# Reordering the state-space stages with a third Toeplitz buffer, moving a copy from GpSimd to ScalarE, and a later softmax sum in a hybrid decoder layer

## The chip, the core and the metric

The kernel runs on one core of a Trainium2 chip. The metric is the device time in microseconds (us) of one execution. Engines are called by the names of the profile: PE is the matmul engine (PEld its weight load), DVE the vector engine, ACT the scalar engine, POOL is GpSimd, and SP issues the transfers.

## The reference, cut to what matters

One decoder layer of 1024 tokens and width 1024. An input projection feeds three token mixers and their gates; then come cross attention and a SwiGLU. Two of the mixers matter here.

```
# forgetting attention, 8 heads x 64
s = q k^T * scale + c_q - c_k          # causal
p = softmax(s);  out = p @ v
# diagonal state space (S5), 32 groups of 16 channels, 64 complex states
drive = u @ bbar;  h = scan(abar, drive);  y = Re(h @ c) + d * u
z = gelu(y);  out = z * sigmoid(z @ w_glu + b_glu)
```

All is float32. Large matmuls are done with each operand split in a high part (fp32r) and the rest, so one product is three matmuls (high x high, high x low, low x high).

## The kernel before, in words

The program is written as generators that a planner interleaves. A stage that has to run in order (the "driven" one) issues a piece of its work; after each piece the planner issues ("pumps") some microseconds of filler matmuls, which are projection blocks `pj` from a list of jobs. Each filler block is 48 matmuls of 512 columns, with weights that SP loads (`wr`), ACT rounds to the high part (`wh`) and DVE turns into the low part (`wl`), one to two blocks ahead. Driven stages are given a priority some instructions ahead of the fillers (60 for S5, 10 for the attention, 20 for work put off with `later`). The order on each engine is fixed when the program is built, by that priority and by when inputs are expected to be there; on the chip each engine takes its instructions in that order and waits where one is not ready. Nearly all tiles come from one arena of 50 buffers of 128 x 1024 floats; an instruction that opens a new tile has to wait for the last reader of the buffer's former tile.

**S5.** `s5_main` walks 8 octets of channels through four stages. `s5_prep` (POOL) makes the tables X and Z1 and loads the inputs U; `s5_prep2` makes rotation tables on DVE (CO, SI), transposes X on PE (`s5g`), makes the short kernel (`s5k`), and SP writes it with 8 transfers into a block Toeplitz matrix (`toep`); `s5_body` projects (`s5d`), rotates and scans on DVE and leaves the carried states in `kcs`; `s5_out` multiplies Toeplitz x U and Z1 x `kcs` on PE (`s5y`), then does the gelu on DVE and ACT and stores. In step o of the loop octet o is in prep, o-3 in out, o-1 in prep2 and o-2 in body, issued in this order, with 4.5, 5.4, 2.7 and 4.5 us of filler after each (S5_US = 4.5 times a weight). `toep` and `kcs` have two buffers each.

**Attention.** `fox_main` runs 16 units (4 pairs of heads, 2 halves of the queries, 2 heads) of 4 or 8 key blocks, 96 blocks in all. A block's scores `st` (PE) go through Exp on ACT to `pf`; POOL copies `pf` to the high part of `pt`; DVE subtracts to get the low part; POOL adds `pf` into the row sums `facc`; two matmuls `pv` follow two blocks later. The maxima of the next unit's scores are found meanwhile (`mx` on PE, reductions on DVE to `mc`, transposes `mt` on PE, q tables `q12a`/`q12b` on ACT). At the end of a unit `fox_out` splits `facc` into `ah` (ACT, then DVE); after the second head of a pair a routine put off by 2.0 us sums `ah` over the partitions on PE (`sm`).

Of the kernel before, what the change touches and what calls it, by code (L numbers as in the profile page):

```python
# [13 lines left out]
AF = mybir.ActivationFunctionType  # L14
ALU = mybir.AluOpType
# [51 lines left out]
HG_LAT = 5.0  # L67
FOXL_W = 10.0
FOXL_T = 8.0
EPS = 1e-6  # L70
NEG = -1e30
HG_LEVELS = (1, 2, 4, 8, 16)
# [116 lines left out]
class Trunk:  # L189
# [538 lines left out]
                out.append(piece(i, c))  # L728
        return out + [chain, rows]

    hi_pool = (0, 1, 2, 3)

    def fox_main(self):
        units = self.fox_units()
        pend = deque()
        pre = self.fox_pre(units[0])
        for i, f in enumerate(pre):
            f()
            yield FOX_P[i >= len(pre) - 3]

        def drain(n):
            while len(pend) > n:
                pend.popleft()()

        for ui, un in enumerate(units):
            p, half, h = un
            self.unit = ui
            pre = self.fox_pre(units[ui + 1]) if ui + 1 < len(units) else []
            nj = 4 * half + 4
            per = [[] for _ in range(nj)]  # L750
            if pre:
                body, tail = pre[:-2], pre[-2:]
                w = nj - PRE_END[half]
                per[0].append(body.pop(0))
                b = BUILD[half]
                for i, f in enumerate(body):
                    per[min(b + i * (w - b) // len(body), w - 1)].append(f)
                per[w - 1].append(tail[0])
                per[nj - 1].append(tail[1])
            acc = self.u("facc")[:, 0:512]  # L760
            st = {}
            pf = None
            for j in range(nj):
                q0 = max(0, 128 * j - 512 * half)
                ps = self.psm("st")
                diag = j >= 4 * half
                self.mm(ps[:, q0:512], self.k1[h][:, 128 * j:128 * j + 128], self.q1[h][:, q0:512], True, False)
                self.mm(ps[:, q0:512], self.k2[h][:, 128 * j:128 * j + 128], self.q2[h][:, q0:512], False, not diag)
                if diag:
                    self.mm(ps[:, q0:q0 + 128], self.ident_r, self.mkq_r, False, True)  # L770
                if j % 2 == 0:
                    pf = self.u("pf").rearrange("p (a b) -> p a b", a=2)
                pr = pf[:, j % 2, q0:512]
                self.act(pr, ps[:, q0:512], AF.Exp)
                pt = self.u("pt", F32R).rearrange("p (a b) -> p a b", a=2)
                if j % 4 in self.hi_pool:
                    self.ts(pt[:, 0, q0:512], pr, 1.0, 0.0, ALU.mult, ALU.add, self.nc.gpsimd)
                else:
                    self.act(pt[:, 0, q0:512], pr, AF.Copy)
                self.sub(pt[:, 1, q0:512], pr, pt.bitcast(F32)[:, 0, q0:512])  # L780
                if j == 0:
                    p0 = pr
                elif j == 1:
                    self.add(acc[:, q0:512], p0[:, q0:512], pr, self.nc.gpsimd)
                    if q0:
                        self.ts(acc[:, 0:q0], p0[:, 0:q0], 1.0, eng=self.nc.vector)
                else:
                    self.add(acc[:, q0:512], acc[:, q0:512], pr, self.nc.gpsimd)

                def pv(j=j, q0=q0, pt=pt, un=un, st=st, nj=nj, acc=acc):  # L790
                    p, half, h = un
                    if j == 0:
                        st["o"] = self.psm("pv")
                    for i in range(2):
                        self.mm(st["o"][:, q0:512], self.vst[j][:, 256 * p + 128 * h:256 * p + 128 * h + 128], pt[:, i, q0:512],
                                start=j == 0 and i == 0, stop=j == nj - 1 and i == 1)
                    if j == nj - 1:
                        self.fox_out(un, st["o"], acc)
                pend.append(pv)
                drain(PV_LAG)  # L800
                for f in per[j]:
                    f()
                yield (0.5 + 0.5 * (512 - q0) / 512) * HALF_W[half] * (FOX_E[j - nj] if j >= nj - 2 else 1.0)
        while pend:
            yield 0.5
            drain(len(pend) - 1)
        yield

    def fox_out(self, un, o, acc):
        p, half, h = un  # L810
        b = 64 * h
        s, so = slice(b, b + 64), slice(64 - b, 128 - b)
        hs = slice(512 * half, 512 * half + 512)
        hd = 2 * p + h
        if half == 0 and h == 0:
            self.fy[p] = self.u(f"fy{p}")
        t = self.u("ft")
        self.act(t[s, 0:512], o[so], AF.Copy)
        self.add(self.fy[p][s, hs], o[s], t[s, 0:512])
        ah = self.u("ah", F32R).rearrange("p (a b) -> p a b", a=2)  # L820
        self.split(acc, ah[:, 0], ah[:, 1])

        self.fah.append((hd, ah))

        def sums():
            ps = self.psm("sm")
            todo, self.fah = self.fah, []
            for n, (hd_, a_) in enumerate(todo):
                for i in range(2):
                    self.mm(ps[0:8], self.ohc_r[:, hd_, 0:8], a_[:, i], start=n + i == 0,  # L830
                            stop=n == len(todo) - 1 and i == 1)
            if p == 0:
                self.nc.vector.tensor_copy(out=self.fsum[0:8, hs], in_=ps[0:8])
            else:
                self.add(self.fsum[0:8, hs], self.fsum[0:8, hs], ps[0:8])
        if h == 1:
            self.later(2.0, sums)
        if half == 1 and h == 1:
            self.nc.sync.dma_start(out=self.fy_d[p], in_=self.fy[p])

# [53 lines left out]
    def s5_params(self):  # L894
# [86 lines left out]
        t = tiny()  # L981
# [89 lines left out]
        for n in (1, 3):  # L1071
            fill(ear, eai, 1, n, n + 1)
        self.ear, self.eai, self.eb = ear, eai, eb

        tz, kz = self.u("toep"), self.u("kcs")
        G.memset(tz, 0.0)
        G.memset(kz, 0.0)
        self.toep, self.kcs = ([t[:, 512 * i:512 * i + 512].rearrange("p (g c) -> p g c", g=4) for i in range(2)]
                               for t in (tz, kz))
        self.s5t = tmv  # L1080
        self.s5d, self.r8 = rv[:, 768:800], rv[:, 800:832]
        G.tensor_copy(out=self.s5d, in_=prm[:, 96:128])
# [36 lines left out]
    def s5_prep2(self, o):  # L1119
        nc = self.nc  # L1120
        g0 = 4 * o
        gs = slice(g0, g0 + 4)
        d = self.s5o[o]
        ut, xt, X, Z1 = (d[k] for k in ("ut", "xt", "X", "Z1"))
        cx = self.cx

        def bh(t):
            return t[:, gs].unsqueeze(3).to_broadcast([P, 4, 8, 16])

        def bk(t):  # L1130
            return t[:, gs].unsqueeze(2).to_broadcast([P, 4, 8, 16])


        et = self.u("s5e")
        dt_ = self.u("s5dd")
        CO = et[:, 0:512].rearrange("p (g a j) -> p g a j", g=4, a=8)
        SI = et[:, 512:1024].rearrange("p (g a j) -> p g a j", g=4, a=8)
        tq = self.s5t[:, 1].rearrange("p (g a j) -> p g a j", g=4, a=8)
        ar, ai = bh(self.ear), bh(self.eai)
        br, bi = bk(self.eb[:, 0]), bk(self.eb[:, 1])  # L1140
        self.mul(CO, ar, br)
        self.mul(tq, ai, bi)
        self.sub(CO, CO, tq)
        self.mul(SI, ar, bi)
        self.mul(tq, ai, br)
        self.add(SI, SI, tq)

        gp = self.psm("s5g")
        for g in range(4):
            self.tp(gp[:, 128 * g:128 * g + 128], X[:, g].rearrange("p s h -> p (s h)"))  # L1150

        kp = self.psm("s5k")
        for g in range(4):
            x0 = X[:, g, 7]
            self.mm(kp[0:16, 128 * g:128 * g + 16], x0, cx[:, 0, g0 + g])
            self.mm(kp[0:16, 128 * g + 16:128 * g + 128], x0, Z1[:, g, 0:7].rearrange("p k h -> p (k h)"))
        G1 = xt[:, 0:512]
        self.act(G1, gp, AF.Copy)
        kt = ut[0:16, 512:1024]
        self.act(kt, kp[0:16], AF.Copy)  # L1160
        tz = self.toep[o % 2]
        ktv = kt.rearrange("p (g c) -> p g c", g=4)
        for s in range(8):
            nc.sync.dma_start(out=tz[16 * s:16 * s + 16, :, 16 * s:128], in_=ktv[:, :, 0:128 - 16 * s])
        d.update(et=et, dt=dt_, G1=G1.rearrange("p (g c) -> p g c", g=4), tz=tz)
# [56 lines left out]
    def s5_main(self):  # L1222

        self.s5o = {}
        for o in range(11):
            for lag, stage in ((0, self.s5_prep), (3, self.s5_out), (1, self.s5_prep2), (2, self.s5_body)):
                if 0 <= o - lag < 8:
                    stage(o - lag)
                    yield S5_W[lag] * (S5_END if o > 8 else S5_BEG if o < 2 else 1.0)
# [968 lines left out]
```

## Time and profile before

| | |
|---|---|
| median of 3 runs | 2164.51 us (2163.9 to 2166.4) |
| the profiled execution | 2162.11 us, span 2160.2 us |
| PE busy | 2101.3 us, 97% of the span |
| DVE / ACT / POOL busy | 1435.6 / 773.0 / 436.0 us |
| granted PE clock, mean | 0.995 |

The span is what the profiler saw from the first to the last instruction; 1.9 us of the execution lie around it. A busy time is the sum over instructions of an engine. S5 runs in the stretch up to about 325 us, the attention from there to about 632 us, and fillers run through both.

### The profile page before, as it was taken

The numbers are of one execution on the slowest core, as the hardware profiler recorded it, in microseconds if no ns is written. First come the engines' busy times: TensorE is split into PE (matmuls) and PEld (weight loads), VectorE is DVE, ScalarE is ACT, GpSimd is POOL, SyncE is SP. The second block draws the span as 40 slices with busy tenths as digits, with TensorE's granted clock in tenths as the row PEclk, the third lists the DMA queues.
The fourth block names the chain that finished last, engine by engine and source line by source line (L and its number), as shares of the span: only waits on it lengthen the run. The fifth ranks groups of instructions, "written<-read, shape, count | busy, mean of one in ns | idle before, by whom it ended". The sixth has DMA issues, their size and how long they took to land.

```text
span 2160.2 us, 26363 instructions
## 1 busy us (share of the span) xinstructions
PE 2101.3 (97%) x10176; PEld 1726.1 (80%) x10176; DVE 1435.6 (66%) x2193; ACT 773.0 (36%) x1208; POOL 436.0 (20%) x399
## 2 busy tenths in 40 slices
PE   8998999999999999999999999999999999989999
PEld 6887776776788888887888888878788888878887
DVE  8887898889845566536665577656877777743421
ACT  4113355545421222227243455444333333341200
POOL 4271204554531111001512000022211111100000
PEclk9999999999999999999999999999999999999999
DMA  4332220111210111124433433152222221272311
GB/s 164 137 99 73 51 86 20 42 47 32 77 63 20 50 69 54 64 108 175 146 104 140 185 98 119 58 184 99 88 88 88 88 80 69 86 273 83 117 58 55
DMA packets 74781, 201.87 MB, mean 93 GB/s; under 512 B 13337, under 2 KB 23065, under 8 KB 74657
## 3 DMA queue, kind: packets, MB, share of 16 engines
q1 hardware_dynamic: 74656, 200.20, 26.7%
q8 instruction: 80, 1.31, 0.2%
q14 instruction: 45, 0.36, 0.1%
HBM read 155.99 MB, written 42.99 MB: 92 GB/s over the span
## 4 chain that ended last, share of the span: by engine, by line
PE 67%; DVE 3%; issue 1%; ACT 1%; POOL 0%; DMA 0%; POOLq 0%; DVEq 0%; SPq 0%; ACTq 0%
PE pj L222 43%; PE fp L222 17%; PE hs L222 2%; PE xo L222 1%; PE xs L222 1%; PE rs L222 1%; PE ho L222 1%; POOL t L240 0%; PE hst L222 0%; DVE wl L240 0%; PE pv L222 0%; DMA wr<-xv 0%; PE st L222 0%; PE xt L227 0%; DVE tl L240 0%
## 5 line engine op out<-in xcount | busy, mean ns | idle before, releaser
L222 PE MATMUL pj<-xl,wh 128*128 128x512 f32 x784 | 315.2, 406 | 3.9 <-DVE xl L252 3.9
L222 PE MATMUL pj<-xh,wh 128*128 128x512 f32 x784 | 312.3, 403 | 6.5 <-ACT xh L237 5.6
L222 PE MATMUL pj<-xh,wl 128*128 128x512 f32 x784 | 311.4, 401 | 0.0
L240 DVE TENSOR_TENSOR wl<-wr,wh 128x1024 fp32r<-128x1024 f32 (+3 forms) x162 | 193.2, 1194 | 52.3 <-ACT wh L237 50.2
L222 PE MATMUL fp<-th,wc 128*128 128x512 f32 x640 | 208.2, 391 | 2.3 <-ACT th L237 2.3
L237 ACT ACTIVATE wh<-wr 128x1024 fp32r<-128x1024 f32 (+3 forms) x162 | 155.1, 960 | 142.1 <-PE pj L222 61.2
L240 DVE TENSOR_TENSOR xr<-pj,xr 128x512 f32<-128x512 f32 x80 | 54.8, 689 | 193.6 <-PE pj L222 188.1
L222 PEld LDWEIGHTS pj<-xh,wh 128*128 128x128 f32 x784 | 148.6, 190 | 39.0 <-ACT xh L237 6.0
L222 PEld LDWEIGHTS pj<-xl,wh 128*128 128x128 f32 x784 | 148.7, 190 | 36.0 <-DVE xl L252 6.1
L222 PEld LDWEIGHTS pj<-xh,wl 128*128 128x128 f32 x784 | 149.2, 190 | 31.0 <-issue 2.2
L222 PE MATMUL fp<-fx,wc 128*128 128x512 f32 x720 | 173.0, 389 | 0.0
L222 PEld LDWEIGHTS fp<-fx,wc 128*128 128x128 f32 x720 | 135.2, 188 | 28.1
L222 PEld LDWEIGHTS fp<-th,wc 128*128 128x128 f32 x640 | 121.0, 189 | 27.9 <-ACT th L237 2.7
L222 PE MATMUL pj<-hh,wl 128*128 128x512 f32 x352 | 134.4, 392 | 3.9 <-DVE wl L240 3.9
L222 PE MATMUL pj<-hh,wh 128*128 128x512 f32 x352 | 133.9, 391 | 1.6 <-ACT wh L237 1.6
L222 PE MATMUL pj<-hl,wh 128*128 128x512 f32 x352 | 133.8, 390 | 0.0
L222 PE MATMUL fp<-tl,wc 128*128 128x512 f32 x320 | 125.3, 392 | 1.5 <-DVE tl L240 1.5
L240 POOL TENSOR_TENSOR fc<-fc,fs 128x512 f32<-128x512 f32 x40 | 57.1, 1428 | 321.8 <-ACT fs L237 210.0
L240 DVE TENSOR_TENSOR pt<-pf,pt 128x512 fp32r<-128x512 f32 (+1 forms) x96 | 94.8, 990 | 39.6 <-POOL pt L256 39.3
L240 POOL TENSOR_TENSOR acc<-acc,sq 128x512 f32<-128x512 f32 (+1 forms) x18 | 30.7, 1707 | 375.8 <-ACT sq L237 375.7
L256 POOL TENSOR_SCALAR pt<-pf 128x512 fp32r<-128x512 f32 (+1 forms) x96 | 67.6, 705 | 139.1 <-ACT pf L237 127.8
L237 ACT ACTIVATE fs<-fc 128x512 f32<-128x512 f32 x40 | 25.3, 633 | 158.9 <-DVE fc L240 154.4
(415 smaller groups left out, 4744.4 us busy)
## 6 DMA issues: line engine op xcount, KB each, us to landing
wr<-w_in SPq DMA_DIRECT2D x48, 512.0 KB, 4.3
wr<-w_gu SPq DMA_DIRECT2D x44, 512.0 KB, 4.6
h_d<-fc SPq DMA_DIRECT2D x22, 512.0 KB, 2.9
hr<-h_d SPq DMA_DIRECT2D x22, 512.0 KB, 5.1
gz_d<-gz SPq DMA_DIRECT2D x20, 512.0 KB, 2.9
gate<-gz_d SPq DMA_DIRECT2D x20, 512.0 KB, 3.7
wr<-xo SPq DMA_DIRECT2D x17, 512.0 KB, 4.8
xr<-x_d SPq DMA_DIRECT2D x16, 512.0 KB, 6.2
```

What stands on the lines that cost most here:

```text
L222: self.nc.tensor.matmul(out, lhsT, rhs, start=start, stop=stop)
L237: self.nc.scalar.activation(out=out, in_=in_, func=f, **kw)
L240: return (eng or self.nc.vector).tensor_tensor(out=out, in0=a, in1=b, op=op)
L256: (eng or self.nc.vector).tensor_scalar(out=out, in0=a, scalar1=s1, scalar2=s2, op0=op0, **kw)
```

## The change

In `s5_main` the order within a step becomes prep (octet o), prep2 (o-1), out (o-3), body (o-2). The Toeplitz matrix of an octet goes to one of three buffers instead of two; the third is half of a new arena tile, `toep2`, cleared by POOL as the others are. In the attention the high part of `pt` is always copied by ACT (before, the set `hi_pool` sent all four residues of j, so every block, to POOL). The softmax sums are put off by 6.0 us instead of 2.0.

```diff
+SUM_AT = 6.0
...
-    hi_pool = (0, 1, 2, 3)
...
                 pt = self.u("pt", F32R).rearrange("p (a b) -> p a b", a=2)
-                if j % 4 in self.hi_pool:
-                    self.ts(pt[:, 0, q0:512], pr, 1.0, 0.0, ALU.mult, ALU.add, self.nc.gpsimd)
-                else:
-                    self.act(pt[:, 0, q0:512], pr, AF.Copy)
+                self.act(pt[:, 0, q0:512], pr, AF.Copy)
                 self.sub(pt[:, 1, q0:512], pr, pt.bitcast(F32)[:, 0, q0:512])
...
         if h == 1:
-            self.later(2.0, sums)
+            self.later(SUM_AT, sums)
...
-        tz, kz = self.u("toep"), self.u("kcs")
-        G.memset(tz, 0.0)
-        G.memset(kz, 0.0)
+        tz, tz2, kz = self.u("toep"), self.u("toep2")[:, 0:512], self.u("kcs")
+        for t in (tz, tz2, kz):
+            G.memset(t, 0.0)
         self.toep, self.kcs = ([t[:, 512 * i:512 * i + 512].rearrange("p (g c) -> p g c", g=4) for i in range(2)]
                                for t in (tz, kz))
+        self.toep.append(tz2.rearrange("p (g c) -> p g c", g=4))
...
-        tz = self.toep[o % 2]
+        tz = self.toep[o % 3]
...
-            for lag, stage in ((0, self.s5_prep), (3, self.s5_out), (1, self.s5_prep2), (2, self.s5_body)):
+            for lag, stage in ((0, self.s5_prep), (1, self.s5_prep2), (3, self.s5_out), (2, self.s5_body)):
```

## Rows read from the trace of the kernel before

**Rows 1.** The page, busy time, share of the span and instructions.
```profile
PE 2101.3 (97%) x10176; PEld 1726.1 (80%) x10176; DVE 1435.6 (66%) x2193; ACT 773.0 (36%) x1208; POOL 436.0 (20%) x399
```
**Rows 2.** Waits of PE, whole span: us in total, times, longest us.
```profile
PE s5y L222 <- DVE kcs L240: 10.1, 6, 3.3
PE sm L222 <- DVE ah L240: 8.1, 5, 2.3
PE mt L227 <- DVE mc L240: 7.8, 9, 1.7
...
PE st L222 <- ACT q12a L237: 1.4, 3, 0.6
...
PE pv L222 <- POOL pt L256: 0.5, 1, 0.5
```
**Rows 3.** Busy time of each engine by stretch, granted clock, DMA share.
```profile
150.00:325.00 175.00, 163.73 (x843) 133.42 (x843) 151.20 (x250) 66.51 (x94) 33.04 (x27) 0.98 0.25 70
325.00:640.00 315.00, 295.68 (x1415) 233.22 (x1414) 250.00 (x390) 160.11 (x269) 150.37 (x186) 0.99 0.14 46
```
**Rows 4.** PE in order of time around 170 us: start, us.
```profile
168.65 0.49 PE L222 MATMUL s5y<-kcs,s5x 128*128 128x128 f32 x2 [2.61 <-DVE kcs L240]
...
171.67 0.63 PE L222 MATMUL pj<-xl,wh 128*128 128x512 f32 x1
172.10 0.63 PE L222 MATMUL pj<-xh,wl 128*128 128x512 f32 x1
...
173.52 0.39 PE L222 MATMUL pj<-xh,wh 128*128 128x512 f32 x1
173.75 0.40 PE L222 MATMUL pj<-xl,wh 128*128 128x512 f32 x1
```
**Rows 5.** Two stretches of 25 us, columns as in rows 3.
```profile
200.00:225.00 25.00, 21.66 (x104) 18.24 (x103) 22.47 (x44) 5.79 (x11) 1.17 (x2) 0.93 0.10 20
...
500.00:525.00 25.00, 21.85 (x97) 16.81 (x96) 22.87 (x33) 11.26 (x19) 12.00 (x14) 0.93 0.08 22
```
**Rows 6.** PE in order of time: prep2 of one octet, and what follows it.
```profile
144.10 0.60 PE L227 MATMUL s5g<-cst,s5x 128*128 128x128 f32 x4
...
145.71 0.50 PE L222 MATMUL pj<-xl,wh 128*128 128x512 f32 x1
```
**Rows 7.** Waits of the SP queue, 60 to 370 us.
```profile
SPq L1164 <- PE s5y L222: 19.4, 3, 13.8
...
SPq L342 <- PE sm L222: 11.6, 1, 11.6
```
**Rows 8.** Waits of POOL, 140 to 325 us.
```profile
POOL s5x L240 <- DVE wl L240: 35.4, 1, 35.4
```
**Rows 9.** The page: costliest groups (busy us, mean ns), and a weight load's issue (us to landing).
```profile
L240 DVE TENSOR_TENSOR wl<-wr,wh 128x1024 fp32r<-128x1024 f32 (+3 forms) x162 | 193.2, 1194 | 52.3 <-ACT wh L237 50.2
...
L237 ACT ACTIVATE wh<-wr 128x1024 fp32r<-128x1024 f32 (+3 forms) x162 | 155.1, 960 | 142.1 <-PE pj L222 61.2
...
L256 POOL TENSOR_SCALAR pt<-pf 128x512 fp32r<-128x512 f32 (+1 forms) x96 | 67.6, 705 | 139.1 <-ACT pf L237 127.8
...
wr<-w_in SPq DMA_DIRECT2D x48, 512.0 KB, 4.3
```
**Rows 10.** Groups by shape, 325 to 632 us: busy us, mean ns, idle before.
```profile
L240 DVE TENSOR_TENSOR pt<-pf,pt 128x512 fp32r<-128x512 f32 x48 | 62.1, 1298 | 31.0 <-POOL pt L256 30.8
...
L240 DVE TENSOR_TENSOR ah<-facc,ah 128x512 fp32r<-128x512 f32 x16 | 11.8, 740 | 0.2
...
L237 ACT ACTIVATE ah<-facc 128x512 fp32r<-128x512 f32 x16 | 10.0, 626 | 0.7 <-DVE pt L240 0.5
...
L237 ACT ACTIVATE pf<-st 128x384 f32<-128x384 f32 x16 | 7.8, 486 | 17.5 <-PE st L222 17.5
...
L240 POOL TENSOR_TENSOR facc<-facc,pf 128x512 f32<-128x512 f32 x24 | 34.7, 1446 | 4.6 <-ACT pf L237 4.6
```
**Rows 11.** Waits of all engines, 325 to 640 us.
```profile
DVE pt L240 <- POOL pt L256: 39.3, 41, 3.5
```

## The prediction

> **What bounds the kernel now.** I began with the page: PE is busy 97% of the span [rows 1], so only its idle time, 2160.2 - 2101.3 = 58.9 us, and what a lower clock costs can be won; work taken off another engine wins nothing by itself. Then the waits of PE, to see whose they are [rows 2], and the table by stretch, to see where: S5 (150 to 325 us) leaves PE idle 175 - 163.7 = 11.3 us and the attention (325 to 640 us) 315 - 295.7 = 19.3 us [rows 3]. The change touches these two stretches and no other, so 30.6 us is the most that waits can give, plus the clock. The reader should see that three names make most of it: `s5y` waits for `kcs` (10.1 us), `sm` for `ah` (8.1), `mt` for `mc` (7.8). All three are ends of DVE chains, and DVE is busy 151.2 of 175 us (86%) in S5 and 250.0 of 315 (79%) in the attention [rows 3].
>
> A wait costs more than its length where the clock falls behind it. After PE stood 2.61 us for `kcs` the matmuls start 0.43 us apart (171.67 to 172.10), and 0.23 us apart again from 173.52 on [rows 4]; that is the lower of the two levels, 1.2 GHz. From the stretches with a granted clock of 0.93 [rows 5] such a dip costs about 25 x 0.07 = 1.75 us; that is two digits only, and I use 1.6. There are three: behind the 2.61 us wait, behind the longest `s5y` wait (3.3, in 200 to 225), and in 500 to 525, where I put it down to the longest `sm` wait.
>
> **The S5 order.** `s5y` of octet o-3 needs the `kcs` of the body one step earlier. Between the two the planner now puts 4.5 + 4.5 = 9.0 us of filler; with prep2 ahead of out it is 2.7 us more, plus prep2's own work on PE, 145.7 - 144.1 = 1.6 us [rows 6]: 4.3 us more distance, against a longest wait of 3.3. So all six should go. The body keeps its place in the step, and its chain on DVE is no longer than it was; what is new ahead of the next body on DVE is the gelu of out where the rotation tables of prep2 stood. Bounds: 0 (the orders on the engines come out such that nothing is won) and 10.1; I take 9.0, one wait of about 1 us left. The two dips go with it: -3.2, bounds 0 and -3.2.
>
> What the stall hands on: DVE's 151.2 us of work would stand in 175 - 9.0 - 3.2 = 162.8 us, 93% full. Then some other chain through DVE is late (a `wl`, a projection's evacuation). I charge one wait of the longest kind seen here, +3.3; bounds 0 and 12.2, which is all of the gain given back.
>
> **The third buffer.** The transfers of the Toeplitz matrix stood 19.4 us in SP's queue, three times, for the `s5y` that frees one of the two buffers [rows 7], with the input loads, the stores and the weight loads behind them. That goes, but PE never waited for those transfers nor for a weight load behind them, so nothing is won. prep2's eight transfers now stand ahead of out's eight stores; nobody on the chip reads the stores until S5 is over. POOL's additional clearing is one instruction on an engine busy 20% of the span [rows 1]. All three: 0.
>
> The price is in the arena. X of one octet waited 35.4 us for a `wl`, a tile it does not read [rows 8]: all 50 buffers are taken, and one is freed for it. The third Toeplitz buffer holds one more through S5, and prep2 ahead of out holds two more at its peak (inputs and tables of four octets, 8, and rotation tables of two, 4; before, 10 in all). What is pushed back then is filler: a weight load opened late. A block is 48 matmuls at 0.23 us = 11 us, and a load needs 4.3 + 0.96 + 1.19 = 6.5 us to be ready (landing, high part, low part) [rows 9]; opened a block or two ahead it has that time to spare. Bounds: 0, and 6.5 us for each block that gets no lead. I take +3.0, half a block.
>
> **Softmax sums.** The sums come 4.0 us of PE work later; the longest wait is 2.3 us (the dip above), so the 8.1 us go but for a remnant: -7.5, bounds 0 and -8.1; the dip in 500 to 525: -1.6, bounds 0 and -1.6. Only the running sum reads the result, and it is needed after the last unit. The `ah` tiles and the bank are held 4 us longer; a weight load once stood 11.6 us for `sm` [rows 7] and would stand up to 4 us more, inside the lead of a block.
>
> **The copies.** POOL loses 96 instructions, 67.6 us [rows 9]. ACT gains as many: 48 at 0.626 us, the price of the same copy of `facc` to `ah`, and 48 narrower ones at no more than 0.486, the 384-wide Exp [rows 10], 30.0 + 23.3 = at most 53 us. ACT goes from 160.1 to 213 of 315 us, 68%: not a bound. But it takes its instructions in order, and behind each copy stand the q tables, `wh` and the sums' high part. PE waited 1.4 us for `q12a`, three times [rows 2], and some smaller times for others of ACT's; about seven such waits, each 0.63 us longer, are +4.4 at worst, 0 at best; I take +1.5. The `pv` wait for POOL, 0.5 us [rows 2], goes: -0.5.
>
> On DVE, 39.3 us of standing for POOL's copy [rows 11] goes, since the copy now follows its Exp on the same engine instead of queueing behind POOL's sums of 1.446 us [rows 10]. And the subtraction takes 1.298 us against 0.740 for the same shape in `ah` [rows 10], so something of POOL's slows it. The gain shows only where PE waits for DVE: `mt` for `mc`. I take -2.0 of the 7.8, bounds -6 and +2.3 (next paragraph).
>
> How POOL slows it the row does not say, and one way speaks against this part. POOL's sum now starts when Exp ends, the subtraction 0.626 us later. If the two cannot run together, the subtraction stands for the remaining 1.446 - 0.626 = 0.82 us and takes 0.74 + 0.82 = 1.56 instead of 1.298 [rows 10]: 48 x 0.26 = 12.6 us more on DVE, and nine `mt` waits 0.26 longer, +2.3 instead of -2.0. The Trainium skill (SBUF — State Buffer, "SBUF: two separate sides") states such a rule: a DVE operation with two SBUF inputs and a GpSimd operation reading SBUF lock each other out for a whole instruction. 1.298 against 0.740 agrees with it, without telling it from a mere slowing down.
>
> **Sum** against the profiled execution, 2162.1: -9.0 - 3.2 + 3.3 + 3.0 - 7.5 - 1.6 + 1.5 - 0.5 - 2.0 = -16.0, so 2146.1. The median of the runs shown is 2.4 us above that execution: 2148.5.
>
> **The rivals.**
> (a) DVE is the real bound of S5. The wait moves to another matmul: -12.2 is given back in full instead of 3.3, a sum of -7.1, 2157. For it: 86% busy. Against it: `kcs` waits are chains placed too early in PE's order, and a DVE that were full would make PE wait for `wl` too, which it hardly did there.
> (b) POOL's sum holds up the subtraction (above): 4.3 us more, 2153. For it: 1.298 against 0.740.
> (c) Slower: the arena starves the fillers in S5. Three buffers fewer of 50 take the lead from weight loads, each such block costs 6.5 us. With -16.0 - 3.0 = -19.0 from the rest it decides from three blocks on; with four, 26 us, the time is 2172. For it: X waits of 35 us. Against it: those waits were POOL's, and PE stood for none of them.
> (d) More is won: nothing is charged for DVE and the arena, and `mt` gives 6: -16.0 - 3.3 - 3.0 - 4.0 = -26.3, 2138.
> (e) Nothing is changed: the orders, fixed when the program is built, shift elsewhere and eat it all: 2164.
>
> **How the numbers follow.** Forecast 0.40, (a) 0.18, (b) 0.10, (c) 0.13, (d) 0.12, (e) 0.07. The forecast's own range is 2141 to 2156, the term for DVE and the one for the arena each off by its size. From the cases: (c) is left out above and the far end of (d) below, which with every bound at its best (-10.1 - 3.2 - 8.1 - 1.6 - 0.5 - 6) would be 2135; the range is 2133 to 2167. 0.2% is 4.3 us, about what a measurement of this kernel can tell from no change: the bounds are 2160.2 and 2168.8. Faster: the forecast, (b) and (d), and half of (a), 0.71; same: the other half of (a) less a little, (e), and a mild (c), 0.16; slower: the rest of (c), 0.13.
>
> **What would show it.** Right: no `s5y` wait for `kcs` over 1 us, a clock of 1.00 in 150 to 225 us; no `sm` wait; `pt` subtractions that wait for ACT and not POOL; ACT near 213 us in the attention's stretch. (a) would show as `pj` waits for DVE of some 10 us in S5; (b) as `pt` subtractions of 1.5 us; (c) as `pj` waits for `wh` or `wl` with a late `wr` before them. Wrong would make me a wait of PE under a name that is not in the rows above, of 5 us or more.

## The result, and the profile after

The changed kernel takes 2177.22 us (median of 4 runs, 2174.1 to 2179.9), the kernel before 2164.34 us beside it (4 runs): a ratio of 1.0061 [1.0044, 1.0078], some 13 us slower. The forecast was 2148.5 us, and the range ended at 2167. The profiled execution took 2174.09 us, its span 2172.3 us, 12.1 us more than before. This is the page's first line of the changed kernel, then the waits of PE (us in total, times, longest), then its stretches of [rows 3] and [rows 5].

```profile
PE 2107.2 (97%) x10176; PEld 1729.3 (80%) x10176; DVE 1422.3 (65%) x2193; ACT 822.4 (38%) x1306; POOL 379.5 (17%) x304
```
```profile
PE s5y L223 <- DVE kcs L241: 13.3, 5, 5.3
PE rs L223 <- ACT sq L238: 6.6, 2, 4.7
...
PE mt L228 <- DVE mc L241: 4.8, 6, 1.2
...
PE pv L223 <- DVE pt L241: 2.5, 5, 0.7
...
PE st L223 <- ACT q12a L238: 2.0, 4, 0.6
...
PE st L223 <- ACT q12b L238: 1.9, 2, 1.2
...
PE sm L223 <- DVE ah L241: 1.2, 1, 1.2
```
```profile
150.00:325.00 175.00, 156.93 (x797) 128.66 (x796) 140.13 (x227) 61.00 (x84) 31.02 (x25) 0.94 0.23 66
325.00:640.00 315.00, 297.51 (x1433) 233.82 (x1433) 243.14 (x408) 213.07 (x376) 97.52 (x92) 1.00 0.14 46
...
275.00:300.00 25.00, 16.55 (x64) 12.07 (x63) 22.69 (x41) 12.39 (x15) 1.89 (x2) 0.80 0.12 31
500.00:525.00 25.00, 23.73 (x113) 17.63 (x111) 19.55 (x32) 17.80 (x32) 8.10 (x8) 1.00 0.08 22
```

The loss stands in the S5 stretch. PE's idle time there went from 11.3 to 18.1 us and the clock from 0.98 to 0.94, which is 175 x 0.04 = 7.0 us: 13.8 us lost. The attention's stretch gave about 1.8 us of idle time back and some 315 x 0.01 = 3 us of clock (both clocks have two digits only). Over the whole span idle time rose by 6.2 us (65.1 against 58.9) and the mean granted clock fell from 0.995 to 0.992, which is 6.6 us: together 12.8, where the span grew by 12.1. Within some 3 us these two are all there is: span less idle time less span x (1 - mean clock) lies between 2087 and 2093 us in every kernel of this study. So each experiment is given with these two columns.

The attention went much as forecast. `sm` waits 1.2 us instead of 8.1, the clock in 500 to 525 us is 1.00, ACT is busy 213.07 us (forecast 213), `mt` waits 4.8 instead of 7.8. In S5 the `s5y` wait that should have gone has grown to 13.3 us, and PE stands 6.6 us for ACT's `sq` (the normalisation of q and k that fillers bring in), 0.5 us before.

To see why, take an octet (counted from 0) from its first `s5d`, where the body's projection begins on PE, to its first product with `kcs`. What PE does in between, the wait for `kcs` left out, is the distance that the prediction wanted longer; with the wait it is the length of the body's chain. PE of the kernel before, octets 2 and 4:

```profile
178.78 1.16 PE L222 MATMUL s5d<-s5u,s5x 128*128 128x128 f32 x8
...
206.65 0.49 PE L222 MATMUL s5y<-kcs,s5x 128*128 128x128 f32 x2 [3.34 <-DVE kcs L240]
...
232.38 1.05 PE L222 MATMUL s5d<-s5u,s5x 128*128 128x128 f32 x8
...
248.41 0.49 PE L222 MATMUL s5y<-kcs,s5x 128*128 128x128 f32 x2 [1.33 <-DVE kcs L240]
```
After, the same octets, then the product of octet 5:
```profile
175.98 1.05 PE L223 MATMUL s5d<-s5u,s5x 128*128 128x128 f32 x8
...
202.34 0.79 PE L223 MATMUL s5y<-kcs,s5x 128*128 128x128 f32 x2 [5.29 <-DVE kcs L241]
...
228.16 1.05 PE L223 MATMUL s5d<-s5u,s5x 128*128 128x128 f32 x8
...
250.44 0.80 PE L223 MATMUL s5y<-kcs,s5x 128*128 128x128 f32 x2 [3.12 <-DVE kcs L241]
...
280.12 0.49 PE L223 MATMUL s5y<-kcs,s5x 128*128 128x128 f32 x2 [3.73 <-DVE kcs L241]
```

Octet 5 had its `s5d` at 257.67 us before, its product at 269.23 behind 0.90 us of waiting; its `s5d` after is at 258.36. In us:

| octet | distance before | after | chain before | after |
|---|---|---|---|---|
| 2 | 24.5 | 21.1 | 27.9 | 26.4 |
| 4 | 14.7 | 19.2 | 16.0 | 22.3 |
| 5 | 10.7 | 18.0 | 11.6 | 21.8 |

So the longest wait, that of octet 2, grew because PE had less to do ahead of the product: a change of the issue order did not become the same change of the order on PE. Its chain was no later. At octets 4 and 5 the distance did grow, and the chain grew by more. DVE shows where. What stands ahead of the body of octet 4 in its queue is, in both orders, the gelu of octet 3 and the rotation tables of octet 5. In the kernel before, the scans of octet 2, then that gelu and those tables:

```profile
200.16 2.22 DVE L1184 TENSOR_TENSOR_SCAN s5dd<-s5rv,s5dd 128x128 f32<-128x128 f32 x4
...
224.94 1.12 DVE L252 SCALAR_TENSOR_TENSOR s5u<-s5u,s5rv,s5y 128x128 f32<-128x128 f32 x4 [0.93 <-PE s5y L222]
...
234.61 1.29 DVE L240 TENSOR_TENSOR s5e<-s5rv,s5eb 128x512 f32<-128x512 f32 x2 [4.11 <-PE pj L222]
```
After, the scans of octet 2, the body of octet 3 with its scans, the gelu and the tables, and a `wl` ahead of the body of octet 5:
```profile
191.85 4.05 DVE L1181 TENSOR_TENSOR_SCAN s5dd<-s5rv,s5dd 128x128 f32<-128x128 f32 x4
...
216.72 2.10 DVE L241 TENSOR_TENSOR s5dd<-s5d,s5e 128x512 f32<-128x512 f32 x3 [5.01 <-DMA sz_d<-s5u]
...
219.58 1.37 DVE L1181 TENSOR_TENSOR_SCAN s5dd<-s5rv,s5dd 128x128 f32<-128x128 f32 x4
...
231.74 0.35 DVE L253 SCALAR_TENSOR_TENSOR s5u<-s5u,s5rv,s5y 128x128 f32<-128x128 f32 x1 [6.89 <-PE s5y L223]
232.00 2.55 DVE L241 TENSOR_TENSOR s5e<-s5rv,s5eb 128x512 f32<-128x512 f32 x2
...
267.42 1.23 DVE L241 TENSOR_TENSOR wl<-wr,wh 128x1024 fp32r<-128x1024 f32 x1 [4.91 <-ACT wh L238]
```
POOL beside these, one operation before and two after, then ACT ahead of the `wh` of that `wl`:
```profile
199.76 1.39 POOL L240 TENSOR_TENSOR s5tm<-s5rv,s5bx 128x512 f32<-128x512 f32 x1
```
```profile
192.02 1.11 POOL L241 TENSOR_TENSOR s5x<-s5pw,s5bx 128x512 f32<-128x512 f32 x1 [30.83 <-DVE wl L241]
...
232.25 1.75 POOL L241 TENSOR_TENSOR s5x<-s5x,s5tm 128x512 f32<-128x512 f32 x1
```
```profile
265.38 0.60 ACT L238 ACTIVATE s5x<-s5g 128x512 f32<-128x512 f32 x1 [4.02 <-PE s5k L223]
```

Beside POOL's tables DVE is slow: the four scans of octet 2 take 4.05 us, where those of octet 3, with no POOL beside them, take 1.37. But this is not new there: in the kernel before POOL waited 35.4 us for the buffer [rows 8], began at about the same time, and held up the same body. At octet 4 two things are new. The gelu of octet 3 begins at 231.74 instead of 224.94, behind a wait of 6.89 us for its `s5y`, which the change had moved later (47.7 us behind the `s5d` of octet 3 instead of 37.1): before, it began 7.4 us ahead of the `s5d` of octet 4, after, 3.6 us behind it. And POOL's tables now fall onto the rotation tables (2.55 us for two operations that took 1.29). At octet 5 DVE stood 4.91 us for a `wh`, which ACT made behind a copy of prep2, for which it stood 4.02 us. The body of octet 3 could not begin until the store of octet 2 had landed (5.01 us), since its tile `s5dd` opens in that octet's buffer; PE did not wait for its `kcs`. In all, DVE's waits for `s5y` grew most. Waits of DVE from 150 to 325 us, after and before:

```profile
DVE s5u L253 <- PE s5y L223: 13.0, 5, 6.9
```
```profile
DVE s5u L252 <- PE s5y L222: 4.6, 4, 1.9
```

e2 and e18 below, which share the S5 part, show the same waits at the same octets (5.4 to 5.5, 3.1 and 3.7 us on PE, 6.9 to 7.1 on DVE). No run takes the causes at octets 4 and 5 apart, so how much each is worth stays open.

The stores themselves stand longer in SP's queue. Over the waits of SP from 60 to 370 us they stand 60.5 us, eight times, where they stood 30.2, seven times, before.

**What POOL does to DVE** the subtraction shows one by one. Of the kernel before, first DVE, then POOL:
```profile
358.16 1.76 DVE L240 TENSOR_TENSOR pt<-pf,pt 128x512 fp32r<-128x512 f32 x1 [1.72 <-POOL pt L256]
```
```profile
358.09 1.29 POOL L240 TENSOR_TENSOR facc<-facc,pf 128x512 f32<-128x512 f32 x1
```
After, DVE without and with POOL beside it, then POOL:
```profile
348.23 0.69 DVE L241 TENSOR_TENSOR pt<-pf,pt 128x512 fp32r<-128x512 f32 x1 [1.59 <-ACT pt L238]
...
402.38 1.14 DVE L241 TENSOR_TENSOR pt<-pf,pt 128x512 fp32r<-128x512 f32 x1
```
```profile
401.68 1.30 POOL L241 TENSOR_TENSOR facc<-facc,pf 128x512 f32<-128x512 f32 x1 [2.03 <-ACT pf L238]
```
Alone it takes 0.69 us. Beside POOL's sum it ends 0.54 us after the sum does, in both kernels (358.16 + 1.76 against 358.09 + 1.29; 402.38 + 1.14 against 401.68 + 1.30): it stands until POOL's instruction is over. Of 18 subtractions of the kernel after that a sum of POOL had begun before, 16 end 0.54 to 0.56 us behind it; beside the other two the sum took longer, 2.72 and 3.53 us, and ended last. By shape, after (busy us, mean ns, idle before):
```profile
L241 DVE TENSOR_TENSOR pt<-pf,pt 128x512 fp32r<-128x512 f32 x48 | 48.3, 1014 | 28.0 <-ACT pt L238 27.9
```
The mean fell from 1298 ns [rows 10] to 1014, since POOL's sum now begins earlier and part of it is over.

### The profile page after: what moved, and what is told of

Its sections match the earlier page's. It is cut to its first block, busy times and chain, and to the rows that moved or that the text cites. A ratio compares the mean times of both kernels' runs of the same rounds, so it can differ in the third digit from the quotient of the medians.

```text
span 2172.3 us, 26433 instructions
## 1 busy us (share of the span) xinstructions
PE 2107.2 (97%) x10176; PEld 1729.3 (80%) x10176; DVE 1422.3 (65%) x2193; ACT 822.4 (38%) x1306; POOL 379.5 (17%) x304
## 4 chain that ended last, share of the span: by engine, by line
PE 69%; DVE 3%; issue 1%; ACT 1%; POOL 0%; POOLq 0%; DVEq 0%; ACTq 0%
PE pj L223 44%; PE fp L223 17%; PE hs L223 2%; PE xo L223 1%; PE rs L223 1%; PE xs L223 1%; PE ho L223 1%; PE st L223 0%; PE pv L223 0%; POOL t L241 0%; PE hst L223 0%; PE xt L228 0%; DVE tl L241 0%; PE fb L223 0%; DVE wl L241 0%
## 5 line engine op out<-in xcount | busy, mean ns | idle before, releaser
L241 DVE TENSOR_TENSOR pt<-pf,pt 128x512 fp32r<-128x512 f32 (+1 forms) x96 | 72.0, 755 | 40.5 <-ACT pt L238 40.3
L241 POOL TENSOR_TENSOR facc<-facc,pf 128x256 f32<-128x256 f32 (+1 forms) x64 | 73.1, 1142 | 121.3 <-ACT pf L238 111.4
```

The source lines that it names most:

```text
L241: return (eng or self.nc.vector).tensor_tensor(out=out, in0=a, in1=b, op=op)
```

## The experiments

All are compared with the kernel before, run beside them on the same chip (its medians 2162.8 to 2164.6 us); nothing of the computation is left out. Idle is span less PE's busy time; idle and clock are those of the profiled execution, which in e10 took 6 us more than the median.

| run | median us | ratio [95%] | idle us | clock |
|---|---|---|---|---|
| before | 2164.3 | | 58.9 | 0.995 |
| after | 2177.2 | 1.0061 [1.0044, 1.0078] | 65.1 | 0.992 |
| e1 copies + sums | 2168.6 | 1.0020 [1.0007, 1.0032] | 60.7 | 0.994 |
| e2 S5 part | 2190.1 | 1.0120 [1.0099, 1.0140] | 72.3 | 0.988 |
| e3 third buffer | 2174.5 | 1.0048 [1.0030, 1.0067] | 67.3 | 0.991 |
| e4 body before prep2 | 2179.4 | 1.0076 [1.0055, 1.0097] | 66.8 | 0.993 |
| e5 arena of 49 | 2188.8 | 1.0110 [1.0087, 1.0134] | 74.9 | 0.988 |
| e6 new order, packed | 2184.1 | 1.0095 [1.0072, 1.0117] | 69.9 | 0.990 |
| e7 products later | 2178.3 | 1.0067 [1.0046, 1.0088] | 65.7 | 0.990 |
| e8 control | 2161.8 | 0.9997 [0.9985, 1.0008] | 61.0 | 0.997 |
| e9 a buffer freed | 2165.5 | 1.0011 [1.0001, 1.0021] | 60.2 | 0.994 |
| e10 e1 with e9 | 2168.9 | 1.0028 [1.0016, 1.0039] | 59.7 | 0.990 |
| e11 copies | 2160.4 | 0.9985 [0.9975, 0.9995] | 57.0 | 0.995 |
| e12 sums | 2171.9 | 1.0035 [1.0021, 1.0049] | 64.0 | 0.993 |
| e13 tables after out | 2185.8 | 1.0109 [1.0094, 1.0124] | 72.2 | 0.990 |
| e14 tables before out | 2167.1 | 1.0021 [1.0012, 1.0030] | 61.3 | 0.994 |
| e15 ah held | 2163.8 | 1.0008 [0.9997, 1.0019] | 59.2 | 0.995 |
| e16 copies, sums at 4.0 | 2166.4 | 1.0023 [1.0012, 1.0034] | 58.6 | 0.993 |
| e17 old order, packed | 2174.1 | 1.0046 [1.0029, 1.0063] | 65.8 | 0.992 |
| e18 change, sums at 2.0 | 2173.1 | 1.0047 [1.0032, 1.0062] | 64.3 | 0.992 |

**The two halves: e1** has the changes of the attention alone (of the diff ahead of the prediction the first four hunks), **e2** those of S5 alone (the last three).

> Only the copies on ACT and the later softmax sums; S5 in the old order with two Toeplitz buffers. If the loss of the full change is all in S5, this is faster than before: the sm waits (8.1 us) shrink to about 1, mt waits from 7.8 to about 5, the clock dip behind the sum goes (1.6), waits for ACT grow by about 2: some 2154 us. A rival in which the ACT copies cost as much as the sums win gives 2162 to 2166.

> Only the S5 order and the third Toeplitz buffer; copies on POOL, sums after 2.0 us. If the loss is all in S5 and the attention's part is a gain of about 10 us, this is the slowest of all, 2183 to 2188 us, with s5y waits of 13 us and a clock of about 0.94 in 150 to 325 us. If the parts act on each other, 2170 to 2177.

Both are slower, the attention's by 4 us, about what can be told from no change, S5's far more (26 us), and S5's half is slower than the whole change. e2 has the waits of the changed kernel, `s5y` 13.5 us and `rs` 6.9.

**The third buffer alone, e3**, in the old order.
```diff
+        self.toep.append(tz2.rearrange("p (g c) -> p g c", g=4))   # tz2: a new arena tile
...
-        tz = self.toep[o % 2]
+        tz = self.toep[o % 3]
```

> The third Toeplitz buffer (one more of the 50 buffers held through S5) with the old order of stages and everything else as before. Theory A, the arena: the one buffer already makes S5 tiles open late, 2168 to 2175 us. Theory B, where the S5 chains fall among POOL's bursts decides, not buffers: 2162 to 2167.

10 us slower. One wait makes most of the added idle time (8.4 us): PE stood 6.47 us at 195.59 for a `wh`, which ACT could not make for want of its load. PE, ACT, then SP of e3 in order of time:

```profile
195.59 0.80 PE L222 MATMUL pj<-wh,xh 128*128 128x512 f32 x1 [6.47 <-ACT wh L237]
```
```profile
194.48 1.06 ACT L237 ACTIVATE wh<-wr 128x1024 fp32r<-128x1024 f32 x1 [9.63 <-DMA wr<-w_v]
```
```profile
178.23 2.50 SPq L1165 DMA_DIRECT2D toep<-s5u  x4
183.51 3.59 SPq L1220 DMA_DIRECT2D sz_d<-s5u  x8
187.14 3.27 SPq L1165 DMA_DIRECT2D toep<-s5u  x4
190.51 0.53 SPq L342 DMA_DIRECT2D wr<-w_v  x1
```
SP of the kernel before in the same place:
```profile
175.45 3.59 SPq L1219 DMA_DIRECT2D sz_d<-s5u  x8
180.74 5.05 SPq L1164 DMA_DIRECT2D toep<-s5u  x8
185.84 1.06 SPq L342 DMA_DIRECT2D wr<-w_v  x2
```
With a third buffer the transfers of the Toeplitz matrix need not wait for the `s5y` of two octets before, so the planner put four of them ahead of the stores; the queue then stood for the gelu behind them, and the weight load behind that went out at 190.51 instead of 185.84. Whether this or the arena buffer costs the time, e17 tells (below). The changed kernel itself does not have this wait: there PE waits 4.1 us for `wh`, as before.

**Where s5y stands: e4** issues the body ahead of prep2 (old tiles), **e7** gives the matmuls of out a later priority in the changed kernel.
```diff
-  ((0, self.s5_prep), (3, self.s5_out), (1, self.s5_prep2), (2, self.s5_body))
+  ((0, self.s5_prep), (3, self.s5_out), (2, self.s5_body), (1, self.s5_prep2))
```
```diff
-        for g in range(4):          # e7, in s5_out
-            self.mm(c, tz[:, g], U[:, g], True, False)
...
+        self.ahead(-40, products)   # products() holds these matmuls
```

> Before, with the order prep, out, body, prep2: the same added distance between body and out as in the change, two Toeplitz buffers, and a peak of 10 S5 buffers with 8 after a step. Theory A: the distance works once the buffers are there, s5y waits of at most 2 us, 2152 to 2156. Theory B: s5y still waits 8 us or more for a body that POOL slows, 2160 to 2172.

> The full change with the matmuls of s5_out issued at a priority 100 instructions later than now (40 behind the program's place instead of 60 ahead). If the s5y waits for kcs (13.3 us and the clock dips behind them) are the loss, they go and this is 2158 to 2165. If they are only where a late S5 chain shows, S5 ends as late as before and the time stays 2172 to 2180.

e4 does what the prediction wanted of the order: `s5y` waits only 4.0 us in all. It is 16 us slower; PE waits 9.9 us for `sq` instead of 0.5. e7 is a weaker test than was expected of it: the call stands inside the stage's own 60, so these matmuls went from 60 instructions ahead to 20 ahead, and not to 40 behind. It left the order all but unchanged, and `s5y` waits 13.2 us. That the planner had nothing else to put there is a reading that it does not show.

**The arena: e5** has 49 buffers instead of 50 (before otherwise), **e9** frees one in S5 (a single `kcs` in spare columns of other tiles), **e10** is e9 with the attention's changes, **e8** a control that only shifts a priority.
```diff
-NSLOT = 50
+NSLOT = 49          # e5
-AH_S5 = 60
+AH_S5 = 56          # e8
-        tz, kz = self.u("toep"), self.u("kcs")
+        tz, kz = self.u("toep"), rv[:, 512:1024]          # e9
```

> The kernel before with 49 arena buffers instead of 50, nothing else. Theory A (the third Toeplitz buffer costs by the arena buffer that it holds through S5): the same order of loss as the third buffer alone, 2170 to 2180 us, with the last s5y some 10 us later than 312.5. If what counts is something else of the third buffer (its clearing, the transfers of the tables), 2162 to 2167.

> The kernel before with one arena buffer freed through S5: kcs has one buffer in the free part of the s5rv tile, and two small tables move beside it. Order of stages, copies and sums as before. Theory A says that S5 is held by the 50 buffers; one buffer less cost 24 us and one held longer 10 us, so one more should end S5 earlier than 312.5 us and give 2152 to 2161 us. If 50 are just enough, 2162 to 2167. If the single kcs makes bodies wait for the products before them, 2168 or more.

> The copies on ACT and the later sums, and one arena buffer freed in S5, old order. If the parts add, the result is that of the freed buffer plus 4 us (the attention's part alone was 1.0020). If the attention's part only needed room, 2150 to 2158. If S5's gain is given back later, 2164 to 2170.

> Control: the kernel before with the S5 stages 56 instead of 60 instructions ahead, no other edit. If a shift of the order costs nothing by itself, 2161 to 2168. If the constants fit this one order so closely that any shift costs about as much as the parts of the change, 2170 or more.

One buffer of 50 less costs 24 us, one more in S5 gives nothing, nor does it help the attention's changes (e10 is 6 us slower than before, e1 4). The control is the same, so not every shift of the order costs.

**The order without a buffer more: e6** puts the third Toeplitz matrix in the second half of `kcs`, which is then single. **e17** has these tiles in the old order. **e13** is e6 with the rotation tables left behind out; **e14** is the kernel before with only these tables ahead of out.
```diff
+        self.toep.append(self.kcs.pop())
...
-        kc = self.kcs[o % 2]
+        kc = self.kcs[0]
```
```diff
+                if lag == 3 and 0 <= o - 1 < 8:
+                    self.s5_tables(o - 1)   # et, dt_, CO, SI out of prep2: e13 after out, e14 ahead of it
```

> The new S5 order with three Toeplitz buffers, but the third takes the half of the kcs tile and kcs has one buffer, so that no arena buffer more is held for it; copies on POOL, sums after 2.0 us. Theory A for the buffer and a cost of the order of its own: about 2190 less the 10 us of the third buffer alone, 2178 to 2183. If the whole loss of the S5 part were the one buffer, 2160 to 2166. If the single kcs makes bodies wait, above 2190.

> The old order (prep, out, prep2, body) with the tiles of the packed runs: three Toeplitz buffers and a single kcs in the room of the four before, so no buffer more. It tells whether the packed runs (2184 to 2186 us) lose by the order or by the single kcs. Theory 1, the order: 2160 to 2170, with s5y waiting about 10 us as before, and the S5 stretch (150 to 345 us) within 4 us of its idle time and clock. Theory 2, the single kcs, which the body may write only when the product of the octet before has read it: 2178 or more.

> The packed order (prep, prep2, out, body with three Toeplitz buffers in the room of the old four), which took 2184.1 us, but with the rotation tables (tiles et and dt) opened after out, where the kernel before has them. Theory 1, the price of the order is the buffers that it holds: two fewer are held at the peak, so S5 ends before 316 us again and the time is 2162 to 2172. Theory 2, the price is the order in which PE, ACT and SP get prep2's other work (transposes, short kernel, eight transfers) ahead of out: the time stays at 2180 to 2188 with S5 ending at 317 us or later. Theory 3, the price is the mere shift of the whole plan: 2170 to 2180, with waits of PE under new names.

> The kernel before, in which only the rotation tables of prep2 (tiles et and dt, six operations of DVE) are made ahead of out. Two more buffers are held at the peak, and nothing else is moved. Theory 1 (buffers): S5 ends at 318 us or later and the time is 2175 to 2185. Theory 2 (the rest of the order): within 4 us of 2164. It also puts the tables on DVE where the whole change has them; if s5y still waits 10 us or more for kcs, the gelu of out was not what stood ahead of the body.

e17 refutes both of its theories: no buffer more, the old order, and yet it is as slow as e3. It has e3's wait in e3's place; PE of e17:
```profile
194.82 0.80 PE L222 MATMUL pj<-wh,xh 128*128 128x512 f32 x1 [6.59 <-ACT wh L237]
```
Up to that load SP's queue is in the order of e3. A single `kcs` costs next to nothing (e9 has it too). So a buffer held more is not needed for e3's loss, and the third Toeplitz matrix, with the queue that it reorders, is what the two share. e6 and e13 are 10 and 12 us slower than e17: that is the order's share, and it is not the place of the tables, since e13 leaves that as it was; alone, the tables ahead of out cost 4.5 us (e14), though `s5y` then waits only 6.1 us. Waits of PE in e13:
```profile
PE rs L222 <- ACT sq L237: 10.8, 4, 6.7
PE s5y L222 <- DVE kcs L240: 6.7, 4, 3.1
```

**The parts of the attention: e11** has the copies alone, **e12** the sums at 6.0 alone, **e15** sums at 2.0 with `ah` held to 6.0 by a read of one element on POOL, **e16** the copies with sums at 4.0, **e18** the whole change with sums at 2.0.
```diff
-            self.later(2.0, sums)
+            self.later(6.0, sums)                      # e12
...
             self.later(2.0, sums)
+            self.later(6.0, lambda: hold(held))        # e15: POOL reads one element of each ah
```

> Only the high parts copied by ACT; sums after 2.0 us, S5 as before. If the copies relieve DVE (39 us of standing for POOL) and the later sums hold buffers for nothing, 2158 to 2163; if the copies are what costs the 4 us of the attention's part (ACT at 68%, new waits of PE for ACT and for what stands behind it), 2168 to 2174.

> Only the softmax sums put off by 6.0 us instead of 2.0. If the sm waits of 8.1 us are a loss of their own, 2154 to 2158. If PE stands there because nothing else is ready, so that the wait comes back under another name, 2162 to 2167.

> The kernel before with sums at 2.0 us as they were, but the two ah tiles of each pair held until 6.0 us by a read of one element on POOL. Theory 1, later sums cost through the buffers they hold: 2168 to 2173, as with the sums at 6.0 (2171.9). Theory 2, they cost through the order on PE, where they stand before other work: 2162 to 2166, with sm still waiting about 8 us in all.

> ScalarE's copies (2160.35 us by themselves) with the sums put off by 4.0 us. Theory 1, later sums cost in proportion to the delay: half of 7.6 us more, 2164. Theory 2, they cost when the order happens to put them before something that is late: anything from 2158 to 2168, and sm's wait (2.7 + 1.6 us with the copies alone) falls under 2 us.

> The changed kernel with the sums put off by 2.0 us again. Alone, the later sums cost 7.6 us. Theory 1, the parts add up: 2177 - 8 = 2166 to 2171. Theory 2, the parts do not add up, since each shifts the order for the others (the S5 part alone took 2190, more than the whole change): 2172 or more, with sm waiting 4 us or more again.

The copies gain 0.15%, less than the 0.2% that a measurement here can tell well, but with an interval below 1; e11 is the fastest version that was run. The later sums cost 7.6 us. Holding `ah` costs nothing that shows (e15), which leaves their place on PE. Waits of PE in e12:
```profile
PE pv L222 <- DVE pt L240: 4.3, 6, 1.4
PE mx L222 <- DVE pmx L703: 3.2, 1, 3.2
PE hst L222 <- ACT hbT L237: 3.0, 1, 3.0
PE pv L222 <- POOL pt L256: 1.2, 2, 0.8
PE sm L222 <- DVE ah L240: 0.9, 1, 0.9
```
7.2 us of `sm` went, and 11.7 us stand under four names that had 0.5 before. At 4.0 us (e16) the loss beside the copies is about as large.

## Why the prediction was wrong, step by step

**The s5y term, -9.0 and the dips -3.2, failed first.** The prediction put `s5y` 4.3 us later in the issue order, took this for 4.3 us more on PE at every octet, and took its partner, the chain on DVE, as no longer than before. Measured: +3.2 us of `s5y` and, in the stretch, 7 us more of clock. The distance on PE changed by anything from -3.5 to +10.7 us (3.1 in the mean of the eight octets), and fell at the longest wait. Where it grew by 4.5 and 7.4 us (octets 4 and 5), the chain grew by 6.3 and 10.2. The step had named the gelu of out as new ahead of the next body, but not that the gelu needs the very `s5y` that is moved later: DVE, in order, stood 13.0 us for it instead of 4.6. And where the wait does go (e4), PE waits elsewhere: it is not worth its length.

**"All three: 0" for the third buffer failed as well.** It asked whether PE waits for the transfers that are freed, not what is moved behind what in SP's queue. Alone this is +10 us (e3, e17): a weight load 4.7 us later, PE 6.5 us idle. In the changed kernel that wait is absent, so how much of the +10 is in its 13 us is not shown. That "nobody on the chip reads the stores" is true of their data, but the next tile waits for the buffer that they read.

**The arena, +3.0.** Rival (c) came nearest in time (2172), and e3 shows its sign, a `pj` wait for `wh` with a late load; but e17 shows the same without the buffer, so the cause that (c) gave is not shown for it. In the changed kernel the sign of (c) is absent: `pj` waits 4.1 us for `wh` and 4.4 for `wl`, 4.1 and 5.8 before. The arena is steep on one side, 24 us for one buffer of 50 (e5), flat on the other (e9). Two tiles opened earlier, with the work on DVE that fills them, cost 4.5 us (e14), near the term; no run shows the +3.0 by itself.

**DVE give-back, +3.3, and rival (a):** refuted as a bound. DVE is busy 140.1 of 175 us, 80% against 86% before [rows 3]: it stands for `s5y`, for `wh` and for a store, and is late, not full.

**The sums, -7.5 and -1.6:** the wait and the dip in 500 to 525 us went as forecast, the gain did not. In the kernel before, +7.6 us (e12); in the changed one, about +4 us (e18 against the change, whose intervals overlap).

**The copies:** ACT's term +1.5 measured 2.1 (`q12a` +0.6, `q12b` +1.5); `mt` -3.0 for -2.0; `pv` now waits 2.5 us for DVE instead of 0.5 for POOL. Alone -3 us (e11), where these three terms made -1.0.

**Rival (b)** was right in its mechanism and wrong in its sum. DVE does stand until POOL's instruction is over (0.54 us beyond its end, above). The Trainium skill (SBUF — State Buffer, "SBUF: two separate sides") states this rule, and the trace agrees. But the 1.298 us of before was a mean over subtractions of 0.69 and of 1.76, so it held the whole wait already; after, the wait is shorter (a mean of 1014 ns).

**The parts do not add up.** e3 +10, the order on top of it +16 (e2 less e3), copies -3, sums +8 make +31; the change is +13. Beside the new S5 order the copies are worth 17 us (e2 2190.1, e18 2173.1), though they lie in another stretch. Half of it is idle time of PE in the attention itself: from 325 to 650 us PE is idle 24.2 us in e2 and 16.3 in e18, 19.3 before and 14.9 in e11. By which chain is open. So is the one through which the order alone costs 10 to 16 us; what is shown is where it lands, PE standing for `kcs` and `sq`, and the clock behind it.

## What to carry to other kernels

A wait in an order that is written out ahead may be a place where the planner had nothing better; before moving it, ask what the waiting side's own chain waits for, and whether that chain, on an engine that works in order, stands behind a reader of the very result that is moved. Write out every queue that the moved step's transfers pass, weight loads behind them above all. A distance in the issue order is not one on the engine: read it from the trace. The length of a wait is not the gain from removing it (in e12 7.2 us of `sm` went, and 7.6 us were lost): measure, with that wait removed alone, whether the time is handed to another name. Buffers come free when the last reader is done, and a store is a reader.

## What the runs showed of the hardware

A DVE operation with two inputs beside a POOL operation with two inputs did not slow down, it stood: the 128x512 subtraction took 0.69 us alone and 1.76 us where POOL's sum had begun 0.07 us earlier, ending 0.54 us after it. In S5 four scans beside POOL's tables took 4.05 us instead of 1.37. A mean of such a group says little; the single instructions do. And of the 12.1 us lost, half was idle time of PE and half the granted clock behind it (0.995 to 0.992 in the mean, 0.80 in the stretch where PE was busy 16.55 of 25 us).
